# Norm factors along the free axis by two transfers through DRAM, and the last squares on VectorE

## The chip, the cores and the metric

The kernel runs on one core of a Trainium2 chip. The metric is the device time of one execution in microseconds, as a median of three runs. One core has five engines with queues of their own: TensorE (PE in the profile; PEld are its weight loads), VectorE (DVE), ScalarE (ACT), GpSimd (POOL) and SyncE (SP). SP and POOL issue nearly all DMA transfers here, POOL through the queue that the profile calls software_dynamic.

## The reference

Two layers of a decoder over 256 tokens of width 2048, all in float32. What matters here is where a norm stands:

```python
def _rmsnorm(x, g):
    xf = x.astype(jnp.float32)
    y = xf * lax.rsqrt(jnp.mean(xf * xf, axis=-1, keepdims=True) + EPS)
    return (y * g.astype(jnp.float32)).astype(x.dtype)

def _conv_ffn(h, w_up, w_conv, b_conv, w_down):
    u = h @ w_up
    gate, val = jnp.split(u, 2, axis=-1)
    ...                     # causal depthwise convolution of gate, width 3
    return (jax.nn.silu(acc) * val) @ w_down

def _finish_layer(x, heads, w_o, norms, w_up, w_conv, b_conv, w_down):
    x = x + _rmsnorm(heads @ w_o, norms[1])
    f = _conv_ffn(_rmsnorm(x, norms[2]), w_up, w_conv, b_conv, w_down)
    return x + _rmsnorm(f, norms[3])
```

Layer 0 projects `_rmsnorm(x, norms[0])` to queries, keys and values of dilated window attention (with rotary positions) and to queries of an attention into 256 memory tokens. Layer 1 projects `_rmsnorm(x, g_kv)` to shared keys and values and `_rmsnorm(x, norms[0])` to its own queries (stick-breaking attention, memory attention). Both layers end in `_finish_layer`.

## The kernel before

**Products and splits.** Weights come in pieces of 128 x 2048 float32 (`raw`, loaded by SP). ScalarE writes a rounded high part into `w` (L755), VectorE the remainder (L756), in halves of 1024 columns, with four `w` tiles in rotation. TensorE multiplies high by high and the two mixed products. The activations `h` are split the same way and are kept transposed, features on the partitions and tokens along the free axis, with the gain g multiplied in but not the norm factor. The factor, one number per token, is multiplied into the product afterwards.

**Two forms of product.** Where the output has tokens on the partitions (`as_mm`, L140), the factor is a per-partition scalar, `r` (128 x 2, token t * 128 + p at [p, t]). Where the output has features on the partitions (`ws_tile`, L179: a matmul of 512 columns and one of 256 per contraction tile, 16 tiles; `ws_sum` adds the two halves of the bank, L190 on ScalarE and L191 on VectorE), tokens lie along the free axis, and the factor is needed as `R`: 128 x 256, the same row in each partition.

**From r to R.** `rstd` sums the collected squares (L270, VectorE) and raises them to the power -0.5 on POOL (L272). `spread` then multiplies, for each half of the tokens, `r` broadcast along 128 columns by the identity matrix on TensorE (L284) and copies the bank to `R` with VectorE (L287). Four spreads make an `R` for 256 tokens of x, and I call their places by letters:

- A, layer 0's input norm (about 84 us into the span). `R`, and `Rs` = R * SCALE (L1239), are multiplied into the rotary tables (L1243, L1244) and the memory queries (L399).
- B, layer 0's MLP (about 385 us). The gate of each MLP tile is multiplied by R in `gate` (L1014), then comes the convolution: L965 on ScalarE, L972 on VectorE.
- C, layer 1's shared norm (about 1112 us): `Rs` (L1239), then keys and queries (L219, L1371).
- D, layer 1's MLP (about 1451 us), as at B.

A fifth spread, of the memory tokens' factor `Rm`, stands apart and is not touched.

**What sets the order.** A planner puts the instructions of each engine into one queue, by its own estimates of when each could run. `later(n, fn)` hangs a small job on the n-th weight piece from there (`step()` runs what is due). `issue_after(ins)` keeps what is made inside it behind an instruction, and `pin` or `keep_in_program_order` keep the written order. POOL's queue also carries the second half of each sum of weights (L763, `first_sums`: a DMA that adds into a tile), `xout` (x set aside to DRAM, L922), the gains of the output norms (L612, broadcast to 128 partitions) and tiles set aside (L705: mk, mv, v).

**The end.** The last piece of the last MLP product is taken as two halves of 256 columns. Each is added to y (L1121), and squared and summed by ScalarE (L278) into a column of `ss`. `finish` reduces `ss` (L270), POOL takes the power (L272), VectorE multiplies y by its gain (L1128), adds y * r to x in four chunks (L626), and SP sends each chunk out (L1480).

Of the kernel before, what the change touches and what calls it, by code (L numbers as in the profile page):

```python
# [10 lines left out]
F32 = mybir.dt.float32  # L11
# [6 lines left out]
P = 128  # L18
D = 2048
S = 256  # L20
# [29 lines left out]
class Body:  # L50
# [138 lines left out]
    def ws_sum(self, out, b):  # L189
        self.pin(self.nc.scalar.copy(out, b[:, S:]))  # L190
        self.pin(self.nc.vector.tensor_add(out, b[:, 0:S], out))  # L191

# [87 lines left out]
    def spread(self, r, name):  # L280

        b = self.bank("s")
        for t in range(2):
            self.nc.tensor.matmul(b[:, t * P:(t + 1) * P], r[:, t:t + 1].to_broadcast([P, P]),  # L284
                                  self.ident, start=True, stop=True)
        R = self.sb.tile([P, S], F32, name=name, tag=name, bufs=1)
        self.nc.vector.tensor_copy(R, b[:, :S])  # L287
        return R

# [617 lines left out]
    def ffn(self, layer, h, each, filler=None, done=None, late=None, early=None, begun=None):  # L907
# [7 lines left out]
        def rms():  # L915
            with self.tc.issue_after(self.last_hi.ins):
                rx = self.x_rstd()
                nc.vector.tensor_scalar_mul(ss[:, :, 4], self.mean, EPS)
            R.append(rx)

            for t in range(2):
                nc.gpsimd.dma_start(self.xout[t], self.x[:, t, :])  # L922

        def spread():
            if len(R) == 1:
                R.append(self.spread(R[0], "R"))
            return R[1]

# [83 lines left out]
        def gate(ga):  # L1012
            Rb = spread().unsqueeze(1).to_broadcast([P, 2, S])
            self.pin(nc.vector.tensor_tensor(ga, ga, Rb, op=ALU.mult))  # L1014

        def narrow(g):
            for p in (2 * g, 2 * g + 1):
# [10 lines left out]
                if p == 0:  # L1028

                    val = self.ws_pair(up[w, 1], h)  # L1030
                gate(ga)
                c, steps = conv(p, ga)
# [101 lines left out]
        if not filler:  # L1134
# [3 lines left out]
            for t in range(2):  # L1138
                for c in range(3 + (t == 0)):
                    self.as_mm(banks[c], parts[c], lhs, 2, (t,))  # L1140
                    evac(c, t, banks[c][t])
                if t:

                    y = ys[3][:, t, :]
                    nc.vector.tensor_add(y, y, banks[3][t])
                    for i in range(2):
                        b, cols = self.bank(), slice(i * 256, (i + 1) * 256)
                        self.as_mm([b, b], parts[3], acts[last[2]], 0, (t,), cols)
                        add_sum(3, t, b, cols, 3 + 2 * i)
                    finish(3, t)  # L1150
                self.add_normed(ys, r[t], t, lambda c: done(t, c))
# [10 lines left out]
    def run(self):  # L1162
# [65 lines left out]
        def x_squares(i):  # L1228
# [4 lines left out]
            if i == 3:  # L1233
                self.r = self.rstd(ss)

        def spread():
            self.R = self.spread(self.r, "R")
            self.Rs = sb.tile([P, S], F32, name="Rs", tag="Rs", bufs=1)
            nc.vector.tensor_scalar_mul(self.Rs, self.R, SCALE)  # L1239

        def turn():
            for i in range(2):
                nc.vector.tensor_tensor(self.rope[:, 2 + i, :], self.rope[:, i, :], self.Rs, op=ALU.mult)  # L1243
# [9 lines left out]
        for i in range(4):  # L1253
            self.later(2 + i, lambda i=i: x_squares(i))
        self.later(6, spread)
        self.later(7, turn)
# [75 lines left out]
        mk, mv = res["mk"], res["mv"]  # L1332
        def spread_b():
            with self.tc.issue_after(self.last_mm.ins):
                spread()

        self.later(4, spread_b)

# [4 lines left out]
        def last_squares():  # L1343
            last = squares(res["ss"], 1, (2, 3))
            self.r = self.rstd(res["ss"])
            return last

# [234 lines left out]
```

## Time and profile before

| | before |
|---|---|
| median of 3 runs | 2139.98 us (2139.54 to 2140.12) |
| profiled execution | 2140.05 us, span 2138.3 us, mean granted clock 0.999 |
| TensorE busy | 2127.1 us (99%) |
| VectorE busy | 1739.6 us (81%) |
| ScalarE busy | 1362.3 us (64%) |
| POOL busy | 179.0 us (8%) |
| DMA | 539.34 MB, mean 252 GB/s |

Engine rows give busy time and its share of the span. A row of a timeline gives its start in the span, the time to the end of the last instruction merged into it, engine, line, what is written from what, and how many instructions; in brackets stands how long the engine sat idle before it and what ended that. A row of waits gives the total, the number and the longest. A row of windows gives the stretch, its length, the busy time of PE, PEld, DVE, ACT and POOL with counts, the granted clock, the DMA engines' busy share and GB/s. A row of DMA issues gives the transfer, the queue, count, KB of one, and the median time from issue to landing.

### The profile page before, as it was taken

How to read it: one execution, taken by the hardware profiler on the slowest of the kernel's cores; microseconds unless marked ns; L12 is line 12 of the kernel's file. 1: busy time of each engine (PE TensorE's matmuls, PEld its weight loads, DVE VectorE, ACT ScalarE, POOL GpSimd, SP SyncE). 2: the span in 40 equal slices, each digit the busy share in tenths (PEclk: the TensorE clock that was granted, in tenths of full speed). 3: DMA queues.
4: the chain of work that ended last, by engine and by line, in shares of the span. 5: the costliest groups of instructions: out<-in, count | busy, mean ns of one | idle time of the engine just before them, and what ended most of it. 6: DMA issues, size and time to landing. Idle time of an engine off the chain costs nothing. (4 is left out here: it accounts for less than half of the span.)

```text
span 2138.3 us, 29329 instructions
## 1 busy us (share of the span) xinstructions
PE 2127.1 (99%) x10894; PEld 1814.4 (85%) x10894; DVE 1739.6 (81%) x2468; ACT 1362.3 (64%) x2118; POOL 179.0 (8%) x201
## 2 busy tenths in 40 slices
PE   9999999999999999999999999999999999999998
PEld 8888888888888888888888888888888888888887
DVE  7798867997887968788898977579978878687886
ACT  6666756676666666666685655466666756666663
POOL 0000001010101011010111000010101010110110
PEclk9999999999999999999999999999999999999999
DMA  9887457796979979797778744577969798897974
GB/s 368 261 264 250 176 180 266 225 286 227 301 235 287 286 217 305 230 289 262 273 270 271 268 160 174 187 251 226 295 223 301 230 289 266 252 291 221 299 247 183
DMA packets 112350, 539.34 MB, mean 252 GB/s; under 512 B 11344, under 2 KB 11728, under 8 KB 74064
## 3 DMA queue, kind: packets, MB, share of 16 engines
q1 hardware_dynamic: 76320, 446.19, 57.9%
q0 software_dynamic: 35744, 91.24, 21.3%
q8 instruction: 85, 1.39, 0.2%
q14 instruction: 57, 0.47, 0.1%
q10 hardware_dynamic: 144, 0.06, 0.0%
HBM read 510.70 MB, written 26.74 MB: 251 GB/s over the span
## 5 line engine op out<-in xcount | busy, mean ns | idle before, releaser
L756 DVE TENSOR_TENSOR w<-raw,w 128x1024 fp32r<-128x1024 f32 (+3 forms) x859 | 869.4, 1033 | 231.1 <-ACT w L755 229.6
L755 ACT CAST w<-raw 128x1024 fp32r<-128x1024 f32 (+3 forms) x859 | 752.4, 901 | 348.5 <-PE ps_g L140 161.0
L179 PE MATMUL ps_s<-h,w 128*128 128x256 f32 (+1 forms) x3200 | 578.2, 333 | 0.8 <-DVE w L756 0.8
L179 PEld LDWEIGHTS ps_s<-h,w 128*128 128x128 f32 x3200 | 496.5, 188 | 72.3 <-DVE w L756 2.1
L140 PE MATMUL ps_g<-w,sh 128*128 128x512 f32 x2244 | 520.2, 391 | 0.0
L140 PEld LDWEIGHTS ps_g<-w,sh 128*128 128x128 f32 x2244 | 419.2, 188 | 87.1 <-ACT sc L870 0.9
L179 PE MATMUL ps_g<-h,w 128*128 128x512 f32 (+1 forms) x1920 | 340.3, 336 | 0.6 <-DVE h L305 0.3
L179 PEld LDWEIGHTS ps_g<-h,w 128*128 128x128 f32 x1920 | 292.0, 188 | 39.1 <-DVE h L305 0.8
L140 PE MATMUL ps_g<-w,h 128*128 128x512 f32 x932 | 229.9, 390 | 0.0
L756 DVE TENSOR_TENSOR x<-sh,x 128x1024 fp32r<-128x1024 f32 x192 | 227.2, 1220 | 0.1
L140 PEld LDWEIGHTS ps_g<-w,h 128*128 128x128 f32 x932 | 174.3, 188 | 32.9 <-DVE w L756 0.4
L755 ACT CAST x<-sh 128x1024 fp32r<-128x1024 f32 x192 | 193.7, 1053 | 1.0 <-DVE sh L812 1.0
L190 ACT COPY qk<-ps_s 128x256 f32<-128x256 f32 x96 | 35.8, 373 | 190.7 <-PE ps_s L179 190.7
L140 PE MATMUL ps_s<-x,h 128*128 128x512 f32 x552 | 155.0, 389 | 0.0
L763 POOL DMA_DIRECT2D sh<-in_uw_dram x80 | 98.2, 1233 | 643.0 <-DMA sh<-in_uw_dram 311.7
L140 PE MATMUL ps_g<-x,h 128*128 128x512 f32 x528 | 148.2, 389 | 0.0
L140 PEld LDWEIGHTS ps_s<-x,h 128*128 128x128 f32 x552 | 103.6, 188 | 21.5
L140 PEld LDWEIGHTS ps_g<-x,h 128*128 128x128 f32 x528 | 99.1, 188 | 17.1
L191 DVE TENSOR_TENSOR qk<-ps_s,qk 128x256 f32<-128x256 f32 x96 | 40.5, 422 | 69.6 <-ACT qk L190 69.6
L972 DVE SCALAR_TENSOR_TENSOR qk<-qk,cols 128x254 f32<-128x254 f32 (+1 forms) x176 | 80.4, 481 | 12.8 <-ACT qk L965 10.3
L140 PE MATMUL ps_s<-w,h 128*128 128x512 f32 x262 | 73.7, 389 | 0.0
L812 DVE TENSOR_TENSOR sh<-sh,raw 128x512 f32<-128x512 f32 x96 | 66.4, 692 | 3.2
(219 smaller groups left out, 1635.2 us busy)
## 6 DMA issues: line engine op xcount, KB each, us to landing
raw<-in_up_dram SPq DMA_DIRECT2D x96, 1024.0 KB, 7.0
raw<-in_dn_dram SPq DMA_DIRECT2D x88, 1024.0 KB, 5.3
raw<-in_uw_dram SPq DMA_DIRECT2D x78, 768.0 KB, 8.1
sh<-in_uw_dram SPq DMA_DIRECT2D x80, 512.0 KB, 8.7
sh<-in_uw_dram POOLq DMA_DIRECT2D x80, 512.0 KB, 10.5
raw<-in_wqk_a_dram SPq DMA_DIRECT2D x24, 1024.0 KB, 5.0
yout<-sh POOLq DMA_DIRECT2D x32, 512.0 KB, 7.5
raw<-in_wo_b_dram SPq DMA_DIRECT2D x16, 1024.0 KB, 4.9
```

The source lines that it names most:

```text
L140: mm = lambda *o, **k: self.pin(self.nc.tensor.matmul(*o, **k))
L179: mm = lambda *o, **kw: self.pin(self.nc.tensor.matmul(*o, **kw))
L190: self.pin(self.nc.scalar.copy(out, b[:, S:]))
L191: self.pin(self.nc.vector.tensor_add(out, b[:, 0:S], out))
L755: high = self.pin(self.nc.scalar.copy(hi, of))
L756: low = self.pin(self.nc.vector.tensor_sub(lo, of, hi.bitcast(F32)))
L763: self.nc.gpsimd.dma_start(d.rearrange("p (a n) -> p a n", a=2), src[u][:, 1536:].unsqueeze(1).to_broadcast([P, 2, 512]), accum_op=ALU.add)
L812: pin(add(half(e, 0), half(e, 1), half(raw, 0)))
L972: pin(nc.vector.scalar_tensor_tensor(c[:, j, d:], ga[:, j, :S - d], w[i], c[:, j, d:], op0=ALU.mult, op1=ALU.add))
```

## The change

`fan_out` takes the place of `spread` at A, B, C and D. It writes the 256 numbers of `r` to a row in DRAM, a transfer of 256 pieces of 4 bytes, and reads that row into all 128 partitions of `R`, a transfer of 128 rows of 1 KB. POOL issues both, directly behind the power, and the second waits for the first. `Rs` is made by `scale`. At B and D the first gate is held behind the last add of the gate tile (`last_sum`). At the end, the squares of the last 256 columns are summed by one VectorE instruction, which starts from the reduction of the other columns (`part`); the power follows directly.

```diff
--- before.py
+++ after.py
@@ -188,7 +188,7 @@
 
     def ws_sum(self, out, b):
         self.pin(self.nc.scalar.copy(out, b[:, S:]))
-        self.pin(self.nc.vector.tensor_add(out, b[:, 0:S], out))
+        self.last_sum = self.pin(self.nc.vector.tensor_add(out, b[:, 0:S], out))
 
     def ws_beside(self, out, src, h, done=None):
 
@@ -285,6 +285,14 @@
                                   self.ident, start=True, stop=True)
         R = self.sb.tile([P, S], F32, name=name, tag=name, bufs=1)
         self.nc.vector.tensor_copy(R, b[:, :S])
+        return R
+
+    def fan_out(self, r, name):
+
+        there = self.outside.tile([2, P], F32, name=name + "row", tag=name + "row", bufs=1)
+        R = self.sb.tile([P, S], F32, name=name, tag=name, bufs=1)
+        self.nc.gpsimd.dma_start(there.rearrange("t p -> p t"), r)
+        self.nc.gpsimd.dma_start(R, there.rearrange("t p -> (t p)").partition_broadcast(P))
         return R
 
     def x_rstd(self):
@@ -916,15 +924,10 @@
             with self.tc.issue_after(self.last_hi.ins):
                 rx = self.x_rstd()
                 nc.vector.tensor_scalar_mul(ss[:, :, 4], self.mean, EPS)
-            R.append(rx)
+            R.extend((rx, self.fan_out(rx, "R")))
 
             for t in range(2):
                 nc.gpsimd.dma_start(self.xout[t], self.x[:, t, :])
-
-        def spread():
-            if len(R) == 1:
-                R.append(self.spread(R[0], "R"))
-            return R[1]
 
         s, make = self.sums_of_h(h)
         self.later(1, rms)
@@ -1010,7 +1013,7 @@
         place = lambda p: p - 2 * sum(v < p // 2 for v in WIDE)
 
         def gate(ga):
-            Rb = spread().unsqueeze(1).to_broadcast([P, 2, S])
+            Rb = R[1].unsqueeze(1).to_broadcast([P, 2, S])
             self.pin(nc.vector.tensor_tensor(ga, ga, Rb, op=ALU.mult))
 
         def narrow(g):
@@ -1028,7 +1031,8 @@
                 if p == 0:
 
                     val = self.ws_pair(up[w, 1], h)
-                gate(ga)
+                with nullcontext() if p else self.tc.issue_after(self.last_sum.ins):
+                    gate(ga)
                 c, steps = conv(p, ga)
                 at_once(steps)
                 if p:
@@ -1143,11 +1147,19 @@
 
                     y = ys[3][:, t, :]
                     nc.vector.tensor_add(y, y, banks[3][t])
-                    for i in range(2):
-                        b, cols = self.bank(), slice(i * 256, (i + 1) * 256)
-                        self.as_mm([b, b], parts[3], acts[last[2]], 0, (t,), cols)
-                        add_sum(3, t, b, cols, 3 + 2 * i)
-                    finish(3, t)
+                    b = self.bank()
+                    self.as_mm([b, b], parts[3], acts[last[2]], 0, (t,), slice(0, 256))
+                    add_sum(3, t, b, slice(0, 256), 3)
+                    part, v, r[t] = self.small(1), self.small(1), self.small(1)
+                    nc.vector.reduce_sum(part, ss[:, t:t + 1, :], axis=AX.X)
+                    b, cols = self.bank(), slice(256, 512)
+                    self.as_mm([b, b], parts[3], acts[last[2]], 0, (t,), cols)
+                    nc.vector.tensor_add(y[:, cols], y[:, cols], b[:, cols])
+                    junk = self.sb.tile([P, 512], BF16, name="junk", tag="junk", bufs=1)
+                    nc.vector.tensor_tensor_reduce(junk[:, cols], y[:, cols], y[:, cols], 1.0 / D, part,
+                                                   ALU.mult, ALU.add, v)
+                    nc.gpsimd.tensor_tensor(r[t], v, self.mhalf[:, 0:1], op=ALU.pow)
+                    nc.vector.tensor_tensor(y, y, gs[3], op=ALU.mult)
                 self.add_normed(ys, r[t], t, lambda c: done(t, c))
             return
         for c in range(4):
@@ -1232,13 +1244,14 @@
                     self.square_into(self.x[:, i // 2, c * 512:(c + 1) * 512], ss[:, i // 2, c:c + 1])
             if i == 3:
                 self.r = self.rstd(ss)
-
-        def spread():
-            self.R = self.spread(self.r, "R")
+                self.R = self.fan_out(self.r, "R")
+
+        def scale():
             self.Rs = sb.tile([P, S], F32, name="Rs", tag="Rs", bufs=1)
-            nc.vector.tensor_scalar_mul(self.Rs, self.R, SCALE)
+            self.tc.keep_in_program_order(nc.vector.tensor_scalar_mul(self.Rs, self.R, SCALE))
 
         def turn():
+            scale()
             for i in range(2):
                 nc.vector.tensor_tensor(self.rope[:, 2 + i, :], self.rope[:, i, :], self.Rs, op=ALU.mult)
                 nc.vector.tensor_tensor(self.rope[:, i, :], self.rope[:, i, :], self.R, op=ALU.mult)
@@ -1252,7 +1265,6 @@
 
         for i in range(4):
             self.later(2 + i, lambda i=i: x_squares(i))
-        self.later(6, spread)
         self.later(7, turn)
         self.later(5, constants)
         s, make = self.sums_of_h(h)
@@ -1330,11 +1342,7 @@
 
         self.ffn(0, h, lambda c: self.x_T(COL_G["kv"], hk, [c], turned), behind_ffn, late=again)
         mk, mv = res["mk"], res["mv"]
-        def spread_b():
-            with self.tc.issue_after(self.last_mm.ins):
-                spread()
-
-        self.later(4, spread_b)
+        self.later(4, scale)
 
 
         kept = [self.set_aside(t, k) for t, k in ((mk, "mk"), (mv, "mv"))]
@@ -1343,6 +1351,7 @@
         def last_squares():
             last = squares(res["ss"], 1, (2, 3))
             self.r = self.rstd(res["ss"])
+            self.R = self.fan_out(self.r, "R")
             return last
 
         self.fill = [None, None, lambda: squares(res["ss"], 1, (0, 1)), last_squares]
```

On TensorE the queues before and after differ in the eight matmuls of L284 alone. VectorE and POOL change their order at the four places. In the rows below, L756 and L764, L305 and L313, L353 and L361, L1014 and L1017, L972 and L975, L763 and L771, L705 and L713 are the same lines before and after. In brackets stand the counters that an instruction waits for (DMASW are transfers of POOL, DMAHW those of SP).

VectorE at C before: the split of the next weight tile (`w`, three pieces) stands behind the last part of `h`, and R comes after it.

```order
L305 SCALAR_TENSOR_TENSOR h_9608<-sh,cols,h_9608 128x256 [waits Activation_49] x4
L756 TENSOR_TENSOR w<-raw,w 128x128 [waits DMAHW1_49,Activation_49]
L756 TENSOR_TENSOR w<-raw,w 128x896 [waits Activation_49]
L756 TENSOR_TENSOR w<-raw,w 128x1024 [waits Activation_49]
L353 TENSOR_TENSOR sh<-sc,sh 128x4x128 [waits Activation_49]
L287 COPY R<-ps_s 128x256 [waits PE_49]
L756 TENSOR_TENSOR w<-raw,w 128x1024 [waits DMAHW2_49,Activation_49]
L1239 TENSOR_SCALAR Rs<-R 128x256 [waits DVE_49]
```

VectorE at C with the change:

```order
L313 SCALAR_TENSOR_TENSOR h_9606<-sh,cols,h_9606 128x256 [waits Activation_49] x4
L1251 TENSOR_SCALAR Rs<-R 128x256 [waits DMASW3_49]
L764 TENSOR_TENSOR w<-raw,w 128x128 [waits DMAHW1_49,Activation_49]
L764 TENSOR_TENSOR w<-raw,w 128x896 [waits Activation_49]
L764 TENSOR_TENSOR w<-raw,w 128x1024 [waits Activation_49]
L361 TENSOR_TENSOR sh<-sc,sh 128x4x128 [waits Activation_49]
```

`Rs` has moved ahead of the three pieces of `w`, and waits for the second transfer.

VectorE at B before, from the last add of the gate tile (L191; `x` is a split kept for the next stage, `h_3360` the tile of sums):

```order
L191 TENSOR_TENSOR qk<-ps_g,qk 128x256 [waits Activation_49]
L287 COPY R<-ps_s 128x256 [waits PE_49]
L756 TENSOR_TENSOR x<-sh,x 128x1024 [waits DMASW6_49,DMAHW0_49,DMASW5_49,DMASW4_49]
L353 TENSOR_TENSOR h_3360<-qk,h_3360 128x4x128 [waits Activation_49]
L1014 TENSOR_TENSOR qk<-qk,R 128x512 [waits DVE_49]
L756 TENSOR_TENSOR w<-raw,w 128x1024
L736 TENSOR_TENSOR qk<-h_2736 128x512
```

VectorE at B with the change:

```order
L191 TENSOR_TENSOR qk<-ps_g,qk 128x256 [waits Activation_49]
L1017 TENSOR_TENSOR qk<-qk,R 128x512 [waits DMASW4_49]
L764 TENSOR_TENSOR w<-raw,w 128x1024 [waits Activation_49]
L361 TENSOR_TENSOR h_3359<-qk,h_3359 128x4x128 [waits Activation_49]
L975 SCALAR_TENSOR_TENSOR qk<-qk,cols 128x255 [waits Activation_49] x2
```

The gate has moved up to L191, and the split of `x` has moved to a later place (behind the fifth `w` from here). D changes in the same way.

POOL at C with the change; before, the power was followed directly by `v` (L705):

```order
L771 DMA sh<-in_wv_b_dram 128x2x512 [waits DMAHW7_49,DMASW0_49,PE_49]
L771 DMA sh<-in_wv_b_dram 128x2x512 [waits DMAHW0_49,DMASW1_49,PE_49]
L272 TENSOR_TENSOR small<-small,mhalf 128x2 [waits DVE_49]
L294 DMA Rrow<-small 128x2x1 [waits DMASW2_49,Pool_49]
L295 DMA R<-Rrow 128x256 [waits DMASW3_49,DMASW2_49]
L713 DMA v_9794<-sh 128x1024 [waits DMASW4_49,Activation_49]
```

The two transfers stand behind two accumulates and the power, and ahead of `v`.

## The prediction

> **What bounds the kernel now.** I read the page's busy shares first, then the waits of TensorE, then the four places where a spread stands, then the last 10 us.
>
> ```profile
> PE 2127.1 (99%) x10894; PEld 1814.4 (85%) x10894; DVE 1739.6 (81%) x2468; ACT 1362.3 (64%) x2118; POOL 179.0 (8%) x201
> PE ps_s L1190 <- DVE mhalf L1184: 1.0, 1, 1.0
> PE ps_s L179 <- DVE w L756: 0.8, 2, 0.6
> PE ps_g L179 <- DVE h L305: 0.3, 1, 0.3
> PE ps_g L179 <- DVE qk L191: 0.3, 1, 0.3
> L284 PE MATMUL ps_s<-ident,small x16: 270/275/275, 83.9 to 1451.1; 128*128 128x128 f32 x16
> ```
>
> TensorE is busy for 2127.1 of 2138.3 us, and all its recorded waits on another engine sum to 2.4 us. The time is therefore the length of TensorE's queue plus the tail behind its last matmul. Something on VectorE, ScalarE or a DMA counts only where TensorE then waits. The 16 records of L284 are the four spreads (two matmuls each, each seen as two records).
>
> **Part 1: eight matmuls leave TensorE.** In the order listing, these eight are the only difference on TensorE. Their price is read off the pace around one of them (TensorE's timeline at 83 us):
>
> ```profile
> 83.18 0.73 PE L179 MATMUL ps_g<-h,w 128*128 128x512 f32 x3
> 83.52 0.50 PE L179 MATMUL ps_g<-h,w 128*128 128x512 f32 x2
> 83.86 0.60 PE L284 MATMUL ps_s<-ident,small 128*128 128x128 f32 x4
> 84.22 0.82 PE L179 MATMUL ps_g<-h,w 128*128 128x512 f32 x3
> 84.65 0.73 PE L179 MATMUL ps_g<-h,w 128*128 128x512 f32 x3
> ```
>
> A pair of L179 (512 columns, then 256) starts every 0.34 us (83.18, 83.52, 83.86). The spread holds the next pair from 83.86 to 84.22, 0.36 us, and the pair after it takes 0.43 us (84.22 to 84.65), 0.09 us more than usual. That is 0.45 us a spread and **-1.80 us** for four. Bounds: 0.36 and 0.45 a spread, so 1.44 to 1.80. I take the upper one, since the slow pair follows the spread directly.
>
> **Part 2: when R arrives instead.** R now comes by two chained transfers on POOL's queue behind the power that makes it. Here are the powers and the places of the first reader (site A, B, C, D):
>
> ```profile
> 70.62 0.72 POOL L272 TENSOR_TENSOR small<-small,mhalf 128x2 f32<-128x2 f32 x1 [16.00 <-DVE small L270]
> 90.36 0.42 DVE L191 TENSOR_TENSOR sh<-ps_g,sh 128x256 f32<-128x256 f32 x1 [0.81 <-ACT sh L190]
> 373.28 0.72 POOL L272 TENSOR_TENSOR small<-small,mhalf 128x2 f32<-128x2 f32 x1 [5.07 <-DVE small L270]
> 385.80 0.42 DVE L191 TENSOR_TENSOR qk<-ps_g,qk 128x256 f32<-128x256 f32 x1
> 1098.66 0.72 POOL L272 TENSOR_TENSOR small<-small,mhalf 128x2 f32<-128x2 f32 x1 [2.05 <-DVE small L270]
> 1110.39 2.42 DVE L756 TENSOR_TENSOR w<-raw,w 128x128 fp32r<-128x128 f32 x3
> 1441.40 1.09 POOL L272 TENSOR_TENSOR small<-small,mhalf 128x2 f32<-128x2 f32 x1 [10.96 <-DVE small L270]
> 1451.36 0.42 DVE L191 TENSOR_TENSOR qk<-ps_g,qk 128x256 f32<-128x256 f32 x1
> ```
>
> The reader follows L191 at A, B and D and goes ahead of L756 at C. From the end of the power to the reader's turn there are 19.4 us at A (71.34 to 90.7), 12.1 at B (374.00 to 386.1), 11.0 at C (1099.38 to 1110.4) and 9.2 at D (1442.49 to 1451.7).
>
> No transfer of 4-byte pieces is in the trace, so both prices are bounded by POOL's transfers:
>
> ```profile
> mv<-sh POOLq DMA_DIRECT2D x1, 512.0 KB, 2.9
> sh<-in_uw_dram POOLq DMA_DIRECT2D x1, 512.0 KB, 6.1
> sc<-in_gb_dram POOLq DMA_DIRECT2D x4, 256.0 KB, 3.8
> sc<-in_gb_dram POOLq DMA_DIRECT2D x16, 256.0 KB, 4.9
> ```
>
> The first new transfer, 256 pieces to DRAM, lies between mv, a write to DRAM of 128 rows (2.9 us), and one accumulate of L763 issued alone, which has 256 rows (6.1). The second, a broadcast of 1 KB to 128 partitions, is nearest to the gains of L612, broadcasts too (3.8 when each goes alone, 4.9 over all). Together that is 6.7 to 11.0 us, and I take 8, since both move far fewer bytes than their neighbours. At A that is hidden for certain. At B R lands at 380.7 to 385.0, before 386.1. At D it lands at 1449.2 to 1453.5, and at 8 us it is 1450.5, 1.2 us early.
>
> The Trainium skill says in "DMA: Bandwidth & Descriptors", section "Anatomy of one DMA — SWDGE (gpsimd) path", that a POOL transfer takes about 2.0 us plus its bytes at 436 GB/s. An estimate by that page for the pair is 4.3 us, R would be in time at all four places, and the sum below would lose its term for C (2137.4 us). This trace disagrees upwards: its 256 KB gains took 3.8 to 4.9 us, where the page gives 2.6.
>
> **Site C is the narrow one**, because two accumulates are still in POOL's queue:
>
> ```profile
> 1094.12 2.50 POOL L763 DMA_DIRECT2D sh<-in_wv_b_dram  x2
> sh<-in_wv_b_dram POOLq DMA_DIRECT2D x2, 512.0 KB, 8.9
> 1099.00:1111.00 12.00, 11.99 (x53) 9.61 (x52) 11.58 (x23) 12.00 (x24) 0.39 (x1) 1.00 0.86 247
> 1112.47 0.61 PE L284 MATMUL ps_s<-ident,small 128*128 128x128 f32 x4
> 1112.83 11.40 PE L179 MATMUL ps_g<-h,w 128*128 128x512 f32 x64
> ```
>
> The second accumulate is issued at about 1095.4 and lands at about 1104.3. The first new transfer stands behind it and lands at best with it, more likely its own 2.9 us later, at 1107.2. POOL waits for that and then issues the second: 1111.4 with the middle 4.2 us of the gains (1108 to 1115.3 between the bounds: 1104.3 + 3.8, and 1104.3 + 6.1 + 4.9). Queued behind the waiting Rs on VectorE are three pieces of `w` (128, 896, 1024 columns) which TensorE takes next. Rs itself delays them by about 0.2 us. TensorE, 0.45 us earlier without the spread, wants the first at 1112.4 and the 896 columns one pair later, at 1112.7. These are ready about 1.5 us after R (0.2 for Rs, 0.2 for the 128, 1.1 for the 896). So R may land until 1111.2 for nothing, and later costs TensorE one for one: **+0.6 us** with 0.4 added as my allowance for POOL's wake-up and issue, bounds 0 to 4.1.
>
> **Sites B and D: the order on VectorE.** The gate (L1014) now stands directly behind L191, two places ahead of where it was, and the copy of R (0.33 us of VectorE) is gone.
>
> ```profile
> 385.80:409.00 23.20, 23.20 (x135) 20.41 (x135) 23.20 (x42) 17.42 (x26) 1.23 (x1) 1.00 0.59 184
> 1462.53 11.13 PE L179 MATMUL ps_g<-h,w 128*128 128x512 f32 x64 [0.29 <-DVE qk L191]
> ```
>
> VectorE works all 23.20 us behind the gate at B, so a late R would be carried on to the `w` of the next stage, and I count no cover for it. R in time costs nothing there: the same instructions run in another order. At D TensorE waited 0.29 us for an L191 that stood behind L990 and L353; the new order has it earlier. I take **-0.29** (bounds -0.29 and 0). If R is late at D (upper bound 1453.5), up to 1.8 us is lost.
>
> **Part 3: the tail.** The last 256 columns are squared and summed by VectorE, not ScalarE:
>
> ```profile
> 2129.33 0.19 ACT L278 ACTIVATION_READ_ACCUMULATOR junk<-sh 128x1 f32 x1
> 2129.72 0.42 DVE L1121 TENSOR_TENSOR sh<-sh,ps_g 128x256 f32<-128x256 f32 x1
> 2130.24 0.42 ACT L278 ACTIVATE junk<-sh 128x256 bf16<-128x256 f32 x1 [0.72 <-DVE sh L1121]
> 2130.56 0.19 ACT L278 ACTIVATION_READ_ACCUMULATOR junk<-sh 128x1 f32 x1
> 2130.78 0.16 DVE L270 TENSOR_REDUCE small<-sums 128x1 f32<-128x6 f32 x1 [0.63 <-ACT junk L278]
> 2131.03 0.92 POOL L272 TENSOR_TENSOR small<-small,mhalf 128x1 f32<-128x1 f32 x1 [9.13 <-DVE small L270]
> L494 DVE CUSTOM_DVE_ANT_0 sc<-ps_s,mask x4: 419/420/424, 184.9 to 295.6; 128x256 f32<-128x256 f32 x4
> L494 DVE DVE_READ_ACCUMULATOR2_ANT small<- x4: 82/84/88, 185.2 to 296.0; 128x1 f32 x4
> ```
>
> Now, from the start of the last add to the power: 2129.72 to 2131.03, 1.31 us. Changed: the partial reduction needs the square that ended at 2129.52 and runs before the add, in VectorE's wait for TensorE. The add issues its successor after about 0.34 us, the fused instruction (L494 is the same kind at the same width) starts at 2130.06, its sum is read at about 2130.4 to 2130.5, and the power starts 0.09 us later, at about 2130.57: **-0.46 us**. Bounds: -0.46, and -0.2 if the fused instruction only starts when the add has ended and a semaphore has passed. The power, the four L626 and the output transfers follow unchanged.
>
> **Sum**, against the profiled execution's 2140.05 us (span 2138.3, and 1.75 around it): -1.80 - 0.29 - 0.46 + 0.6 = -1.95, so 2138.1. The median shown is 2139.98, 0.07 lower, so **2138.0 us**.
>
> **Rivals.** (a) *The late R takes the gain back*: at C the transfers take their upper bounds (R at 1115.3, +4.1) and at D too (+1.8), so 2139.98 - 1.80 - 0.46 + 5.9 = 2143.6; with half of that loss, 2140.7, no change. For it: a DMA share of 0.86 at C, and 4-byte pieces, which nothing here prices. Against it: few bytes. (b) *POOL is held off*, and the kernel gets slower. POOL can be kept from its operands while VectorE works:
>
> ```profile
> 340.27 3.60 POOL L272 TENSOR_TENSOR small<-small,mhalf 128x1 f32<-128x1 f32 x1
> L763 POOL DMA_DIRECT2D sh<-in_uw_dram x80: 1190/1204/1697, 349.9 to 2029.1; - x80
> ```
>
> One power took 3.60 us, where the fastest took 0.56. If each new transfer met a hold of 3 us, R would be 6 us later than above: about 1117.8 at C (6.6 lost), 1456.5 at D (4.8), 388 at B (1.9): 2139.98 - 2.26 + 13.3 = 2151.0. It decides from about 2 us of hold a transfer. Against it: 80 issues of L763 took 1.70 us at most. The Trainium skill has this rule in "SBUF — State Buffer", "SBUF: two separate sides": VectorE in a two-port mode locks POOL out, and descriptors can't be written; by it the time would be that of this rival, and the row of L763 bears it out weakly at most. (c) *More than the forecast*: even if all of TensorE's waits but the first (1.4 us) vanished too, it is 2139.98 - 1.80 - 1.4 - 0.46 = 2136.3.
>
> **How the numbers follow.** Forecast 0.62, (a) 0.27, (b) 0.07, (c) 0.04. The forecast's own range is 2137.2 to 2139.4. For eight in ten I reach down to (c)'s neighbourhood and up into (a): 2136.8 to 2141.8. A measurement of this kernel can tell about 0.2%, 4.3 us, from no change. Faster by more than that would need more than spreads, tail and waits hold: 0.03. Slower by more is (b) and a piece of (a): 0.08. Within: 0.89.
>
> **What would show it.** In the changed profile: no L284 on `small`, and L179 pairs 0.34 us apart through these places; VectorE's waits name R only at the Rs of C, for about 1 us, with TensorE waiting about 0.6 us for `w` behind it; the power at the end starts about 0.85 us after the last add's start. I am wrong if R is late at B or D, if TensorE's gaps move elsewhere, or if the pair of transfers takes under 6 or over 12 us.

## The result, and the profile after

The changed kernel takes **2159.1 us** (median of 6 runs, 2155.2 to 2159.3) against 2139.8 us for the kernel before beside it: a ratio of 1.0085, 95% interval 1.0075 to 1.0095. It is 19 us slower, where the forecast was 2138.0 us. The profiled execution took 2159.14 us, span 2157.4 us, 19.1 us longer than before's 2138.3.

The page's first part and the waits of TensorE (us in total, times, longest):

```profile
span 2157.4 us, 29309 instructions
PE 2131.4 (99%) x10878; PEld 1814.6 (84%) x10878; DVE 1739.2 (81%) x2466; ACT 1361.2 (63%) x2116; POOL 184.8 (9%) x209
PE ps_g L179 <- DVE w L764: 10.6, 3, 5.5
PE ps_g L179 <- DVE qk L191: 2.7, 1, 2.7
PE ps_s L179 <- DVE w L764: 1.3, 4, 0.4
PE ps_g L140 <- DVE w L764: 0.8, 1, 0.8
PE ps_g L140 <- ACT w L763: 0.4, 1, 0.4
```

TensorE lost the 16 records of the spreads, 10894 to 10878, and yet is busy 4.3 us longer, and it now waits some 17 us where it waited 2.4. VectorE's share did not move. All long waits but one name the remainder `w` that VectorE writes (L764 here, L756 before); the 2.7 us name an add of VectorE's (L191, at D).

Apart from the eight matmuls both kernels issue the same matmuls in the same order, so the lag of one behind the other can be read at any place, as the difference of the starts of the same matmuls (here the median of neighbours). It grows at three of the four places and nowhere else:

| | lag ahead of the place | lag behind it | step |
|---|---|---|---|
| A (82 us, 100 us) | 0.26 | -0.20 | -0.46 |
| B (384, 430) | -0.31 | 3.49 | +3.80 |
| C (1111, 1140) | 3.49 | 11.16 | +7.67 |
| D (1449, 1490) | 11.34 | 18.98 | +7.64 |
| end (2128) | | 18.90 | |

What stands there is the chain of the two transfers. Rows of POOL's and VectorE's timelines at B, C and D (start, us, line; in brackets the idle time ahead and what ended it). L294 issues the first transfer, L295 the second; L1017 is the gate, L1251 makes Rs:

```profile
373.99 0.77 POOL L294 DMA_DIRECT2D Rrow<-small  x1 [0.22 <-POOL sums L263]
383.30 0.58 POOL L295 DMA_DIRECT2D R<-Rrow  x1 [8.54 <-DMA Rrow<-small]
390.18 0.69 DVE L1017 TENSOR_TENSOR qk<-qk,R 128x512 f32<-128x512 f32 x1 [4.27 <-DMA R<-Rrow]
1103.17 0.78 POOL L294 DMA_DIRECT2D Rrow<-small  x1 [0.30 <-POOL small L272]
1114.45 0.59 POOL L295 DMA_DIRECT2D R<-Rrow  x1 [10.50 <-DMA Rrow<-small]
1121.26 0.29 DVE L1251 TENSOR_SCALAR Rs<-R 128x256 f32<-128x256 f32 x1 [7.31 <-DMA R<-Rrow]
1454.13 0.77 POOL L294 DMA_DIRECT2D Rrow<-small  x1 [0.31 <-POOL small L272]
1465.51 0.58 POOL L295 DMA_DIRECT2D R<-Rrow  x1 [10.61 <-DMA Rrow<-small]
1471.80 0.69 DVE L1017 TENSOR_TENSOR qk<-qk,R 128x512 f32<-128x512 f32 x1 [8.68 <-DMA R<-Rrow]
```

From the issue of the first transfer to R's reader it is 16.2 us at B, 18.1 at C and 17.7 at D. The first transfer, 1 KB in 256 pieces, holds POOL for 9.3 to 11.4 us until it can issue the second; the second takes another 6.3 to 6.9. VectorE stands 4.27, 7.31 and 8.68 us ahead of its reader, 20.3 us in all, with the splits of the next weights queued behind.

The DMA engines show what goes on meanwhile. Windows (stretch, length, busy time of PE, PEld, DVE, ACT, POOL, granted clock, share of the 16 DMA engines, GB/s) in the 8 us behind the issue at B, first of before, then of the changed kernel:

```profile
376.00:384.00 8.00, 8.00 (x47) 7.05 (x47) 6.46 (x13) 4.91 (x6) 0.00 (x0) 1.00 0.47 160
```

```profile
376.00:384.00 8.00, 8.00 (x48) 7.05 (x47) 6.46 (x14) 4.91 (x6) 0.58 (x1) 1.00 0.96 55
```

Same work, but the engines are busy for 0.96 of the time and move 55 GB/s, a third of before's. The time is not booked on the small pieces themselves: from 373 to 384 us the weight loads of SP's queue have 96% of the engines' time, POOL's queue has 0.3%. The loads are slowed: the piece that SP issues at 376.60 lands after 11.7 us, where the same piece of the kernel before took 4.8.

There is a second loss, a lower granted clock. Windows of the changed kernel behind the stalls at B, C and D:

```profile
402.00:406.00 4.00, 4.00 (x25) 3.50 (x24) 4.00 (x7) 1.43 (x4) 0.00 (x0) 1.00 0.88 316
1122.00:1126.00 4.00, 4.00 (x12) 3.11 (x13) 4.00 (x5) 0.78 (x1) 0.00 (x0) 0.50 0.58 180
1126.00:1130.00 4.00, 4.00 (x21) 3.45 (x21) 3.64 (x6) 1.05 (x1) 0.00 (x0) 0.83 0.97 373
1480.00:1484.00 4.00, 4.00 (x18) 3.46 (x18) 4.00 (x9) 3.11 (x6) 0.00 (x0) 0.71 0.15 20
```

25 records in 4 us at full clock behind the 2.1 us gap at B; 12 and then 21 behind the 5.45 us gap at C, at a granted clock of 0.50 and 0.83. That is 17 records of 0.16 us, 2.7 us, and it closes the account at C: 5.45 us of gap, 2.7 of slow clock, -0.46 for the spread gives 7.7 against a step of 7.67. At D two gaps (3.05 and 2.69 us) were followed by 18 records at 0.71. The Trainium skill says in "TensorE: Matmul & The Clock Gate", section "Part 1: The HAM clock gate", that an idle window of about 3.4 us halves TensorE's clock. The gaps of 5.45 and 2.1 us agree with it. D's two gaps, each under 3.4 us and with 2.8 us of work between them, do not, nor does a gap of 2.0 us at B in the run below in which ScalarE issues the first transfer: 0.50 was granted for 3.4 us behind it. So the length of a gap does not decide alone here; what else does, no run shows.

The tail is the one part that came nearly as drawn:

```profile
2148.63 0.42 DVE L1157 TENSOR_TENSOR sh<-sh,ps_g 128x256 f32<-128x256 f32 x1 [0.21 <-PE ps_g L140]
2149.08 0.48 DVE L1159 CUSTOM_DVE_ANT_0 junk<-sh,small 128x256 bf16<-128x256 f32 x1
2149.49 0.08 DVE L1159 DVE_READ_ACCUMULATOR2_ANT small<- 128x1 f32 x1
2149.66 1.05 POOL L1161 TENSOR_TENSOR small<-small,mhalf 128x1 f32<-128x1 f32 x1 [9.34 <-DVE small L1159]
```

From the start of the last add to the power it is now 1.03 us, against 1.31 before.

### The profile page after: what moved, and what is told of

The parts are those of the page before. It is cut to its first block, busy times and chain, and to the rows that moved or that the text cites. A ratio compares the mean times of both kernels' runs of the same rounds, so it can differ in the third digit from the quotient of the medians.

```text
span 2157.4 us, 29309 instructions
## 1 busy us (share of the span) xinstructions
PE 2131.4 (99%) x10878; PEld 1814.6 (84%) x10878; DVE 1739.2 (81%) x2466; ACT 1361.2 (63%) x2116; POOL 184.8 (9%) x209
## 4 chain that ended last, share of the span: by engine, by line
PE 86%; issue 6%; DVE 3%; DMA 3%; ACT 1%; POOL 1%; POOLq 0%; SPq 0%; DVEq 0%; ACTq 0%
PE ps_g L140 35%; PE ps_s L179 25%; PE ps_s L140 11%; PE ps_g L179 11%; DVE w L764 1%; DMA Rrow<-small 1%; DMA R<-Rrow 1%; DMA raw<-in_up_dram 1%; PE ps_s L1071 1%; ACT w L763 0%; PE ps_s L423 0%; PE ps_s L450 0%; POOL small L272 0%; DVE x L634 0%; PE ps_s L595 0%
## 5 line engine op out<-in xcount | busy, mean ns | idle before, releaser
L764 DVE TENSOR_TENSOR w<-raw,w 128x1024 fp32r<-128x1024 f32 (+3 forms) x859 | 869.6, 1034 | 227.6 <-ACT w L763 226.2
L763 ACT CAST w<-raw 128x1024 fp32r<-128x1024 f32 (+3 forms) x859 | 752.2, 901 | 346.7 <-PE ps_g L140 163.4
L764 DVE TENSOR_TENSOR x<-sh,x 128x1024 fp32r<-128x1024 f32 x192 | 227.3, 1221 | 0.2
L763 ACT CAST x<-sh 128x1024 fp32r<-128x1024 f32 x192 | 193.6, 1053 | 5.5 <-DVE sh L820 5.5
L771 POOL DMA_DIRECT2D sh<-in_uw_dram x80 | 98.9, 1242 | 634.0 <-DMA sh<-in_uw_dram 285.3
L191 DVE TENSOR_TENSOR qk<-ps_s,qk 128x256 f32<-128x256 f32 x96 | 40.6, 422 | 66.4 <-ACT qk L190 66.4
L975 DVE SCALAR_TENSOR_TENSOR qk<-qk,cols 128x254 f32<-128x254 f32 (+1 forms) x176 | 80.4, 482 | 12.8 <-ACT qk L968 10.4
```

What stands on the lines that cost most here:

```text
L191: self.last_sum = self.pin(self.nc.vector.tensor_add(out, b[:, 0:S], out))
L763: high = self.pin(self.nc.scalar.copy(hi, of))
L764: low = self.pin(self.nc.vector.tensor_sub(lo, of, hi.bitcast(F32)))
L771: self.nc.gpsimd.dma_start(d.rearrange("p (a n) -> p a n", a=2), src[u][:, 1536:].unsqueeze(1).to_broadcast([P, 2, 512]), accum_op=ALU.add)
L975: pin(nc.vector.scalar_tensor_tensor(c[:, j, d:], ga[:, j, :S - d], w[i], c[:, j, d:], op0=ALU.mult, op1=ALU.add))
```

## The experiments

Three theories were put against each other. *Late*: R arrives late at B, C and D, VectorE stands in order ahead of the reader, and TensorE starves. *Pieces*, or *traffic*: the first transfer's small pieces hold the DMA engines, so that R or the weights come late. *Order*: the gate's and Rs's new places cost time whatever makes R. Beside them stood *chain* and *POOL*, by which two dependent transfers, or POOL's queue, take this long whatever they carry.

### The tail alone

Before, with the change's last hunk in `ffn` and nothing else.

```diff
-                    for i in range(2):
-                        b, cols = self.bank(), slice(i * 256, (i + 1) * 256)
...
+                    nc.vector.tensor_tensor_reduce(junk[:, cols], y[:, cols], y[:, cols], 1.0 / D, part,
+                                                   ALU.mult, ALU.add, v)
```

> Before, with the change's tail alone (the last 256 columns squared and summed by one VectorE instruction, started from the reduction of the other columns); the four spreads and the order stay as before. In the changed kernel's trace the way from the start of the last add to the power is 1.03 us, against 1.31 before, so every theory expects -0.28 us here: about 2139.6 us against 2139.8. The prediction's own term was -0.46. If more than 1 us is gained or lost, the tail has an effect on the order of other work that I have not seen.

Measured: 2140.17 us against 2139.81, ratio 1.0003 (0.9995 to 1.0012). The last rows of its timeline:

```profile
2130.01 0.41 DVE L1153 TENSOR_TENSOR sh<-sh,ps_g 128x256 f32<-128x256 f32 x1
2131.03 1.05 POOL L1157 TENSOR_TENSOR small<-small,mhalf 128x1 f32<-128x1 f32 x1 [8.82 <-DVE small L1155]
2132.12 0.75 DVE L626 SCALAR_TENSOR_TENSOR x<-sh,small,x 128x512 f32<-128x512 f32 x1 [0.44 <-POOL small L1157]
```

Add to power is 1.02 us, as in the changed kernel; the power is 0.13 us longer than before's 0.92, so 0.15 us is left at L626 (2.11 us behind the add, 2.26 before). No timing can see that. The tail is not where 19 us came from.

### One site alone, in two ways

Before with the new tail and with `fan_out` at A only. In the first of the two runs Rs was left where `spread` had been called, in the second it is made in `turn`, as in the change:

```diff
-        self.later(6, spread)
+        self.later(6, lambda: spread(True))      # first run: Rs alone is left there
...
         def turn():
+            scale()                              # second run: Rs here, nothing at step 6
```

> Before, with the new tail and with the two transfers at site A alone; B, C and D keep their spread on TensorE. In the changed kernel TensorE went through A without a wait and came out 0.4 us earlier against before than it went in. Theory 'late' (R lands late at B, C and D, and that is the whole cost) expects -0.4 and -0.28: about 2139.1 us, 0.7 under before. Theory 'traffic' (the 4-byte pieces hold up the weight loads, and TensorE pays for late weights) expects A to cost too, as its pieces meet the same weight loads: over 2141 us.

> The run with site A alone once more, with Rs = R * SCALE kept directly ahead of the rotary tables, as the change has it (in the first such run the planner put Rs early in VectorE's queue, and VectorE stood 10.2 us there for R). New tail; B, C and D with their spread on TensorE. Theory 'late' (a reader ahead of R's landing is what costs, and A's reader is now behind it) expects -0.4 for the spread and -0.28 for the tail: 2138.7 to 2139.8 us. Theory 'traffic at every place' (the pieces of 4 bytes at A hold up the weight loads, and TensorE pays) expects 2142 us or more.

The first measured 2146.36 us, ratio 1.0030 (1.0019 to 1.0042), the second 2140.12 us against 2140.04, ratio 0.9997 (0.9989 to 1.0006). The first looked like 'traffic', and its trace says that it was not. Its waits of VectorE and TensorE:

```profile
DVE Rs L1257 <- DMA R<-Rrow: 10.2, 1, 10.2
PE ps_g L179 <- DVE w L764: 4.2, 1, 4.2
```

The planner had put Rs ahead of R's landing; VectorE stood there 10.2 us, TensorE 4.2, and the lag at A is +6.4 us. In the second, VectorE reads R behind its landing, and the lag at A falls by 0.45 us, one spread (as much comes back near 101 us, where I can name no cause). The same pieces of 4 bytes are in both. So at A it was the reader standing too early that cost, and the gain of one spread and the tail is too small to be measured: 2140.12 is 0.3 us over the forecast of 'late', inside the interval.

### R by TensorE again, in the new order

```diff
     def fan_out(self, r, name):
...
+        return self.spread(r, name)
```

> The changed kernel with R made by TensorE again (two matmuls and a copy, called where the two transfers were issued), with its gates, scale and tail left where the change put them. Theory 'order' (the gate directly behind the last add, and Rs ahead of the splits, cost time whatever makes R) expects most of the 19 us to stay: 2150 to 2159 us. Theories 'late' and 'traffic' expect before's time less the tail and at most 0.3 us at D: 2139.2 to 2140 us. A planner's other choices in this build may add a us.

Measured: 2144.08 us against 2139.81, ratio 1.0021 (1.0012 to 1.0030), between the two forecasts. It does not isolate the order, since the spread's matmuls now stand where `fan_out` was called, too early:

```profile
PE ps_s L284 <- POOL small L272: 3.4, 3, 1.8
```

TensorE waits 3.4 us for the power itself, and 2.6 us of its lag appear near 675 us, at none of the four places. The run bounds what the order could cost at 4.3 us; the run with rows below settles it.

### The transfers without a reader

Before, whole, plus the pair behind each power into a tile that nobody reads (the second transfer reads a row of 512 B, half of the change's):

```diff
+            self.fan_out(rx, "U")            # B and D
...
+                self.fan_out(self.r, "U")    # A, and the same at C
```

> Before, with the pair of transfers added behind each of the four powers (256 pieces of 4 bytes to DRAM, then a row of 512 B read into 128 partitions of a tile) and nobody reading the result; the four spreads stay and make R. Nothing of the computation is changed. Theory 'traffic' expects a good part of the loss here: the DMA engines are held for some 7 us at each place, weights come late, 2145 to 2155 us. Theory 'late' expects no change: 2139.5 to 2141 us, with the first transfer taking as long as in the changed kernel (9 to 11 us from its issue to the next issue).

Measured: 2148.75 us, ratio 1.0040 (1.0025 to 1.0056). Nobody waits for R, and still about 9 us are lost, so 'late' alone is refuted as the only cost. By the trace's lag it is 0.0 at A and B, +0.8 at C, +7.7 at D; another 1.7 us appears near 800 us, where no such transfer is, and stays unexplained. Rows at D:

```profile
1445.47 0.77 POOL L294 DMA_DIRECT2D Urow<-small  x1 [0.31 <-POOL small L272]
1457.01 1.05 ACT L763 CAST w<-raw 128x1024 fp32r<-128x1024 f32 x1 [5.73 <-DMA raw<-in_up_dram]
1457.41 0.58 POOL L295 DMA_DIRECT2D U<-Urow  x1 [11.16 <-DMA Urow<-small]
1470.60 9.64 PE L179 MATMUL ps_g<-h,w 128*128 128x512 f32 x40 [4.11 <-DVE qk L191]
1445.40:1457.40 12.00, 12.00 (x73) 10.62 (x72) 6.78 (x14) 4.33 (x6) 0.77 (x1) 1.00 0.81 83
```

ScalarE stands 5.73 us for a weight piece (`raw`) that SP loads, until the first transfer is done: over these 12 us the DMA engines are 0.81 busy at 83 GB/s (before, in the same 12 us of the program: 0.65 at 230). TensorE then stands 4.11 us, and the granted clock behind that is 0.50 for 4 us. So the pieces also reach TensorE by way of the weights, where a load is short of slack. In the changed kernel itself ScalarE's longest wait for a weight piece of that kind is 1.8 us (2.3 before), so there this way cost little: R was late anyway.

### What makes the first transfer long

Four runs keep the change and give the first transfer another shape or another queue (the new tiles and the reading side are left out here). Only with ScalarE's queue does R still hold the factors in their places.

```diff
 # e4_8byte: 128 pieces of 8 bytes
-        there = self.outside.tile([2, P], ...)
+        there = self.outside.tile([P, 2], ...)
+        self.nc.gpsimd.dma_start(there, r)
 # e5_512byte: 128 pieces of 512 bytes
+        there = self.outside.tile([P, P], ...)
+        self.nc.gpsimd.tensor_copy(wide, r[:, 0:1].to_broadcast([P, P]))
+        self.nc.gpsimd.dma_start(there, wide)
 # e6_rows: 2 pieces of 512 bytes
+        self.nc.gpsimd.tensor_copy(row, r[0:2, 0:1].to_broadcast([2, P]))
+        self.nc.gpsimd.dma_start(there, row)
 # e12_act: 256 pieces of 4 bytes, issued by ScalarE
+        self.nc.scalar.dma_start(there.rearrange("t p -> p t"), r)
```

> The changed kernel with the row in DRAM laid out as 128 x 2 instead of 2 x 128: the first transfer has 128 pieces of 8 bytes, not 256 of 4. R then holds the factors in another sequence (each token's product is scaled by another token's factor), which changes no time. Theory 'pieces' (the price of the first transfer is the number of its small pieces) expects its time from issue to the next issue to fall from 9.3 to 11.4 us to about 6, R to land 4 to 5 us earlier, nothing lost at B, about 3 at C and 4 at D: 2144 to 2149 us. Theory 'chain' (two dependent transfers on POOL's queue take this long whatever their pieces) expects 2157 to 2160 us.

> The changed kernel with a first transfer of 128 pieces of 512 bytes: POOL copies the factor of token half 0 along 128 columns, all of it is written to DRAM (64 KB), and the second transfer reads the first two rows of it as R. R's values are not the factors (two rows of one repeated number), which changes no time; POOL has one more copy of about 0.3 us. Same number of pieces as the run with 8 bytes, 64 times the bytes. Theory 'pieces by number' expects the time of that run, 2144 to 2149 us. Theory 'pieces by size' (a piece far under 512 bytes is slow in itself) expects the first transfer to take 3 to 5 us and the time to be near the forecast, 2138 to 2142 us. Theory 'chain' expects 2157 to 2160.

> The changed kernel with a first transfer of 2 pieces of 512 bytes: POOL copies the factors of tokens 0 and 1 along a row of 128, and these two rows go to DRAM and back as R. R's values are not the factors, which changes no time; POOL has one more copy of about 0.3 us. Theories of pieces, by number or by size, expect the first transfer to take 2 to 4 us and the pair 7 to 9, so that the blind forecast's terms hold: 2138 to 2141 us. Theory 'chain' expects 2157 to 2160 us.

> The changed kernel with its first transfer (256 pieces of 4 bytes) issued by ScalarE instead of POOL; the second stays with POOL. If POOL's queue is what makes the first transfer long ('POOL'), the first transfer should take 2 to 4 us, R land in time, and the time be near 2140 us. If the pieces themselves are what takes long, whatever the queue, R is as late as in the changed kernel: 2155 to 2162 us. ScalarE's own wait for the power adds at most 1 us a place in either case.

| first transfer | time, us | ratio to before (95%) | its issue to the next, at A, B, C, D | second, issue to landing (median) |
|---|---|---|---|---|
| 256 x 4 B (the change) | 2159.1 | 1.0085 (1.0075 to 1.0095) | 9.9, 9.3, 11.3, 11.4 | 6.8 |
| 256 x 4 B, by ScalarE | 2156.30 | 1.0076 (1.0063 to 1.0089) | 11.0, 9.9, 12.4, 8.6 | 6.5 |
| 128 x 8 B | 2143.04 | 1.0013 (1.0004 to 1.0022) | 5.5, 6.9, 8.0, 6.9 | 5.9 |
| 128 x 512 B | 2140.67 | 1.0001 (0.9992 to 1.0011) | 4.8, 2.3, 6.9, 7.1 | 3.9 |
| 2 x 512 B | 2140.06 | 0.9999 (0.9990 to 1.0009) | 6.2, 2.4, 6.5, 6.5 | 3.5 |

At B, in the order of the table's last three rows, the second transfer's issue (the first was issued at 373.78, 375.56 and 375.45):

```profile
380.63 0.56 POOL L295 DMA_DIRECT2D R<-Rrow  x1 [6.24 <-DMA Rrow<-small]
```

```profile
377.90 0.56 POOL L297 DMA_DIRECT2D R<-Rrow  x1 [1.73 <-DMA Rrow<-wide]
```

```profile
377.88 0.59 POOL L297 DMA_DIRECT2D R<-Rrow  x1 [1.85 <-DMA Rrow<-row]
376.00:384.00 8.00, 8.00 (x48) 7.05 (x47) 6.46 (x13) 4.92 (x6) 0.62 (x2) 1.00 0.49 177
```

At B, where the engines are otherwise least loaded, 128 pieces of 8 bytes take 6.9 us and 128 pieces of 512 bytes 2.3: the same number, 64 times the bytes, a third of the time. At A, C and D other transfers set a floor of 5 to 7 us for either: with two rows the first transfer lands 0.2 us behind the weight load in flight ahead of it, at all four places (at D at 1448.82, the load at 1448.67). There the 8 bytes show in the second transfer, which queues behind what the first has held up. So take the pair, as the mean of the first over the four sites and the median of the second: 8.9 us with two rows, 9.2 with 128 x 512 B, 12.7 with 128 x 8 B, 17.3 in the change, 17.0 from ScalarE. 128 and 2 large pieces cost nearly the same, so number alone is not it; 128 small ones cost 3.5 us over 128 large ones, 256 small ones 8.1. From these figures I estimate about 30 ns of delay a small piece, or, spread over 16 engines, some 0.5 us a piece on its engine. The run with 8 bytes came out 1 us under the forecast by number. With two rows the DMA engines at B are back at 0.49 busy and 177 GB/s.

ScalarE's queue takes as long as POOL's, and 'POOL' falls. 'Chain' falls with the runs of 512 bytes. So does 'order': the run with rows has the change's order on TensorE and VectorE, instruction for instruction, and loses nothing.

The Trainium skill has this in "DMA: Bandwidth & Descriptors", section "Specifications": at least 512 B a transfer for line rate, below which the engine does a read-modify-write. The runs agree with the bound's side (512 bytes fast, 8 bytes slow); what the engine does inside, and whether the read from SBUF or the write to DRAM is the slow half, no run here shows. One rival is left: the small pieces also lie side by side in DRAM, all of them within 1 KB. No run writes small pieces far apart, so whether their size or their crowding costs stays open.

### How much a late R costs, without small pieces

One or two more links between the write and the broadcast, in the run with rows (e10, e11), and one in the changed kernel (e8):

```diff
         self.nc.gpsimd.dma_start(there, row)
+        self.nc.gpsimd.dma_start(far0, there)
+        self.nc.gpsimd.dma_start(far1, far0)     # e11 only
+        self.nc.gpsimd.dma_start(R, far1.rearrange("t p -> (t p)").partition_broadcast(P))  # far0 in e10
```

> The run with a first transfer of 2 pieces of 512 bytes, with one more link: the row is copied once from DRAM to DRAM before it is read into R. No small pieces; only R is later, by 5 to 7 us, which makes it 13 to 16 us from the power to R against 16 to 18 in the changed kernel. R's values are not the factors, as in that run. Theory 'late alone costs' (VectorE stands in order before the reader, with the splits of the next weights behind it) expects about 1 us at B, 4 at C and 5 at D: 2147 to 2152 us. Theory 'the pieces cost' (it is the DMA engines held by small pieces that TensorE pays for, and a late R alone is mostly covered) expects 2140 to 2143 us.

> The same with two links from DRAM to DRAM: R lands 19 to 22 us after the power, 2 to 4 us later than in the changed kernel, without small pieces. Theory 'late alone costs' expects more than the changed kernel's loss, from the run with one link about 6 us more at each of B, C and D: 2162 to 2172 us. Theory 'the pieces cost' expects 2143 to 2150 us.

> The changed kernel with one more link in the chain: the row of 1 KB is copied from DRAM to DRAM before it is read into R. That makes R later by the time of this copy, I expect 4 to 6 us, with hardly any more traffic. Theory 'late' expects TensorE to pay this once each at B, C and D, some 1 us at A (where the cover is 19.4 us), and a little more through a lower granted clock behind each gap: 2171 to 2180 us. Theory 'traffic' expects no more than 2 us above the changed kernel: 2159 to 2161 us.

Measured: 2149.68 us, ratio 1.0043 (1.0030 to 1.0056); 2156.61 us, 1.0077 (1.0064 to 1.0090); 2168.26 us, 1.0126 (1.0109 to 1.0143). The last two are under their forecasts, in e11 since the second link took only 2.0 to 4.4 us (the first 3.8 to 5.3; the one in e8 4.9 to 7.0), in e8 since its last transfer, which no longer stands directly behind the small pieces, landed in 3.5 us where the change's takes 6.8. VectorE's waits for R in e11 and in e8:

```profile
DVE qk L1023 <- DMA R<-Rfar: 10.3, 2, 7.9
DVE Rs L1257 <- DMA R<-Rfar: 8.4, 1, 8.4
```

```profile
DVE qk L1019 <- DMA R<-Rrow: 19.5, 2, 12.3
DVE Rs L1253 <- DMA R<-Rrow: 11.3, 1, 11.3
```

Set beside the span, all runs with the change's order lie near one line (each span is of one execution; with 8 bytes, executions ran from 2140.6 to 2146.7 us):

| run | VectorE's waits for R, sum | span against before's 2138.3 |
|---|---|---|
| two rows | 2.3 | -0.9 |
| 128 x 512 B | 3.0 | +0.8 |
| 128 x 8 B | 7.2 | +5.7 |
| two rows, one link | 10.3 | +8.4 |
| by ScalarE | 17.6 | +18.1 |
| two rows, two links | 18.7 | +16.7 |
| the change | 20.3 | +19.1 |
| the change, one link | 30.8 | +29.2 |

From the first row to the last that is 30.1 us of time for 28.5 us of wait, about one for one; all but ScalarE's run lie 1 to 3 us under their wait, where the spreads' 1.8 us are. With the two runs of two rows and links, which have no small pieces, 'late' is shown as a cause by itself, of the size that the changed kernel needs: a line through the runs with two rows and with two links gives 18.4 us at the change's 20.3 us of wait, against 19.1. A late R takes about 1 us for each us, the lower clock included.

### What follows

The change's loss is R's lateness at B, C and D, made by the first transfer's small pieces. Pieces without a late reader can cost as well (7.7 us at D in one profile, where a weight load came late, but nothing at A and B). In the changed kernel the two overlap. At D, where the pieces alone cost most, VectorE's wait and TensorE's step in lag can be set side by side: 2.28 and 1.24 us with two rows, 5.51 and 4.47 with one link, 7.87 and 6.92 with two, and 8.68 and 7.64 in the change. The step is the wait less about 1.0 us, with small pieces as without (only ScalarE's run differs, 5.80 and 5.49), so beside a late R the pieces cost nothing more there. No version beats the kernel before measurably: two rows instead of 256 pieces (whose R is not the right one) and site A alone both come out at 1.000.

## Why the prediction was wrong

**The step that failed is the price of the pair of transfers**: 8 us taken, with bounds of 6.7 to 11.0, and 16.2 to 18.1 us measured at B, C and D, from the first issue to R's reader. The second transfer, bounded at 3.8 to 4.9, took 6.3 to 6.9 (3.2 to 4.0 from issue to landing with two rows). The first, bounded at 2.9 to 6.1 by neighbours with 128 and 256 *rows*, took 9.3 to 11.4 to the next issue. The reason given, that both "move far fewer bytes than their neighbours", did not bear: the neighbours' pieces are large, and the runs above show that small ones cost, few bytes or not. The row that a bound is taken from must match in the size of a piece, and no row did, as the prediction itself says; the upper end should have stayed open. "DMA: Bandwidth & Descriptors" of the Trainium skill, which the prediction quotes for a price of 2.0 us plus bytes, also has the bound of 512 B, in "Specifications", and the prediction left that out.

Point by point:

- **Spreads, -0.45 each.** Right: -0.46 at A, and -0.47 at B with two rows.
- **Site C, R may land until 1111.2, then one for one.** Nearly right. The threshold stands 11.8 us behind the power's end, in the changed kernel at 1114.7; R's reader ran at 1121.26, 6.6 us late, and TensorE waited 5.45, so it stood about 1 us too early. One for one left out the clock: 2.7 us more. One reading was wrong: the 8.9 us by which the second accumulate lands at 1104.3 is the median of two, which took 6.75 and 11.1 us, and the second landed at 1106.0.
- **B and D, no cover for a late R.** Right: 4.27 and 8.68 us late cost 4.25 and 8.09 (each step with the spread's 0.45 taken out). That R lands before 386.1 at B and 1.2 us early at D was wrong with the price.
- **-0.29 for TensorE's wait at D.** In the changed kernel that wait is 2.69 us. With two rows it is gone from TensorE's waits, as forecast.
- **Tail, -0.46.** The sum is -0.28 to the power. The fused instruction starts 0.45 us behind the add's start, when the add has ended, not 0.34; that was the other bound's case. The power then took 0.13 us longer.
- **Rival (a), the late R.** The mechanism was right, at 0.27. Its price, 4.1 at C and 1.8 at D, stood on the same bounds and had nothing for B; the three places cost 20.5 us with the spreads taken out, three to four times as much.
- **Rival (b), POOL held off.** Its time was nearest, its reason wrong: both issues took 0.77 and 0.58 us, and the pieces are as slow from ScalarE's queue. The Trainium skill's rule in "SBUF — State Buffer", "SBUF: two separate sides", that VectorE can keep POOL from writing descriptors, shows in none of these issues.

The prediction's own signs of being wrong named what came: R late at B and D, and a pair of over 12 us.

With a first transfer of two rows the forecast's terms can be checked as they stood. The pair took 10.1 us at D (1442.63 to 1452.71), inside the bounds but 2 us over the 8 taken; VectorE waited 2.28 us for R there and nowhere else, and D's step was +1.24 us, where the prediction had given up to 1.8 for its upper bound. About 1.1 us of the wait is POOL's copy, which the change does not have between the power and the first issue (1.45 us, against 0.31 in the change). The time was 2140.06 us, without a difference to before and 2 us over the forecast.

## What to carry to other kernels

Price a transfer by the size of its contiguous pieces before its bytes: 1 KB in pieces of 4 bytes took longer here (10.3 us in the median from issue to landing) than 512 KB in long rows (2.9 and 6.1), and held up the weight loads beside it. When work moves from a busy engine to a chain of transfers, compare the chain's whole latency with the time until the first reader in an in-order queue, since behind that point the lateness is paid in full. If TensorE stands idle for 2 us or more, reckon with a lower clock behind the gap too (2.7 us at C).

## What was not expected of the hardware

- **256 pieces of 4 bytes hold up all the DMA engines.** At B the engines were 0.96 busy at 55 GB/s for 8 us beside a transfer of 1 KB, and loads of another queue crawled (11.7 us for a weight piece instead of 4.8; at D, without a reader, ScalarE waited 5.73 us for one).
- **The clock falls behind a short gap.** 5.45 us idle at C was followed by some 8 us at a granted clock of 0.50, then 0.83, 2.7 us of loss. Of two gaps of about 2 us at B, one was followed by 1.00 (the change, 2.1 us), the other by 0.50 for 3.4 us (issued by ScalarE, 2.0 us).
